# A hybrid decoder step: joining TensorE products that use part of the array, and another order for the first and the middle stretch

## The chip, the cores and the metric

One core of one Trainium2 chip. The time of a kernel is the device time of one execution in microseconds; the median of several runs is compared. All data is float32. "Full" products below use all 128 rows and 128 columns of TensorE's array.

## What is computed

A prompt of 512 rows and 8 sample rows (520 columns in the kernel's transposed layout, called T) go through two layers of width 1024. Cut to what matters here:

```python
def adaln(c, w, b):
    mod = (jax.nn.silu(c) @ w + b)[:, None, :]
    return jnp.split(mod, 3, axis=-1)          # shift, scale, gate

def even_layer(...):                            # layer 0
    h = rmsnorm(x, g) * (1 + scale) + shift
    z = h @ w_in                                # 8192 columns: conv parts, gates, q, k, v
    y_a = short_conv(...) * silu(ga)
    o = dilated_attn_prompt(q, k, v, slopes)    # or _decode, on 1024 cached keys and values
    out = concatenate([y_a, o * silu(gb)]) @ w_out
    return x + gate * out

def odd_layer(...):                             # layer 1
    h = rmsnorm(x, g) * (1 + scale) + shift
    z = h @ w_in                                # 6144 columns: u, gate, q, k, v, gate
    y_c = pool_mix(u, ...) * silu(gc)
    ret_new, o = retention_prompt(q, k, v)      # or retention_chunk on a state of 256 x 256 a head
    out = concatenate([y_c, norm(o) * silu(gd)]) @ w_out
    return x + gate * out
```

Both layers need adaLN's shift, scale and gate of 9 condition rows (8 samples, 1 prompt), and each is a product with a 1024 x 3072 matrix.

## The kernel before

**Tiles.** Activations are held transposed, 8 blocks of 128 features by 520 columns. A "tile" of work is one block of 128 output features: 8 blocks k, and in each three products (`mm3`, lines 295 to 302): high half of the weights by high and by low half of h, low half of the weights by high half of h, each over 256 and 264 columns, so 48 products. Halves come from a rounding on ScalarE (`whi`) and a subtraction on VectorE (`wlo`). Weights stream through four raw, three high and three low buffers (`w_raw`, `w_hi`, `w_lo`), asked for one tile ahead or more, all on SyncE's queue. There are 144 such tiles: 64 of layer 0's input projection, 16 of its output projection, 48 and 16 of layer 1.

**Order of the rest.** Everything else is hung between tiles by a clock written by hand: after each k of a tile `tick` (line 198) runs what is due, from four lists. `at` has fixed times; `put` is a heap of which one entry goes per tick; `put_fill` is a queue that is served when `put` has nothing due; `put2` goes every second tick. So one tick is 6 products of a tile, and the order on each engine is that of the calls. Engines run their own instructions strictly in order; a load on SyncE that waits for a buffer holds the loads behind it.

**What the change touches.**
- `H1A, H1B, DV, DK` (line 89): in ticks, when layer 1's blocks of h are scaled (H1A, and H1B between blocks) and how long the turning of v and k in the first retention head is put off (DV, DK), at the seam between the layers. There the first four tiles of layer 1 work on unscaled x (`z_first`), since the mean square is not known yet; `k_turn` (line 930, transposes on line 933) takes what ScalarE has made of such a tile.
- `ada_mm`, `ada_fin`, `ada` (lines 336 to 366): one adaLN block gives two column blocks. The condition is the stationary side, 32 columns of it, and the four column groups of the array (32 each) work on four k at once; the result is copied (`md`), turned and summed over the groups by a reduce, and its bias is added. Layer 0 has 8 blocks for shift and scale at the beginning and 4 for the gate during mixer A, layer 1 has 8 during the head pairs and 4 during layer 0's output projection. Each block is 1 MB in one of three `big` buffers.
- `score` (line 528) in `head_pair`: for a block of 128 queries and both heads e of a pair, three products each on 64 rows of the array; the two heads use the two halves of the rows. It is called four times a pair (8 pairs), for queries 0 to 3, and `soft` follows for each head.
- `window_weigh` (line 710): the sample rows' attention weights by cached values, on 32 columns of the array, four times.
- `state_read` (line 1054) in `ret_head`: q of the samples by the retention states, on 32 columns, twice a head, for samples 0 to 3 and 4 to 7.
- The beginning (lines 409 to 472): x is loaded, its mean square summed by products with a matrix of ones (`on_d`), the root's reciprocal taken on 520 columns, x multiplied by it on GpSimd, and then, in a loop over the blocks j, the adaLN block j is computed, h of block j - 1 is made, and the first two tiles take in block j - 2.
- `rms_sums`, `rms_roots`, `rms_rows` (lines 384 to 406): another way to the same root, with one-column products; before, only the seam uses it.

A float32 product runs as two passes on TensorE, so a profile counts two instructions for one; the products of tiles and scores are float32r and run as one.

Of the kernel before, what the change touches and what calls it, by code (L numbers as in the profile page):

```python
# [18 lines left out]
P = 128  # L19
D = 1024  # L20
KT = D // P
S = 512
# [64 lines left out]
def hybrid_kernel(ctx: ExitStack, tc: tile.TileContext, a, o):  # L87
    nc = tc.nc
    H1A, H1B, DV, DK = 11, 2, 6, 6
# [270 lines left out]
    def ada(layer, kind, j, raw=None):  # L360
        raw = raw or ada_load(layer, kind, j)

        def first():
            put_fill(ada_fin, layer, kind, j, ada_mm(raw), after=2)

        put_fill(first)
# [59 lines left out]
    sqa = tt()  # L426
# [6 lines left out]
    for x, first in ((sqa, True), (sq, False)):  # L433
        mm(ssq[0][:, 0:H0], on_d, x[:, 0:H0], first, not first)
        mm(ssq[1][:, 0:T - H0], on_d, x[:, H0:T], first, not first)
    act(r0[:, 0:H0], ssq[0][:, 0:H0], ACTF.Sqrt, bias=eps[:, 0:1])
    act(r0[:, H0:T], ssq[1][:, 0:T - H0], ACTF.Sqrt, bias=eps[:, 0:1])
    nc.vector.reciprocal(r0[:, 0:H0], r0[:, 0:H0])
    nc.vector.reciprocal(r0[:, H0:T], r0[:, H0:T])
    for x in xT:  # L440
        nc.gpsimd.tensor_tensor(out=x, in0=x, in1=r0, op=ALU.mult)
    for layer in range(2):
        o0 = PV[f"ada{layer}"] + 8
        vts(bsc[layer], pv[:, o0:o0 + 8], 1.0, None, ALU.add)
    h0, w01, ps01, hx = [], [], [mm2(), mm2()], {}

    for j in range(KT + 2):
        if j < KT:
            md = ada_mm(raw0[j])
        if 0 < j <= KT:  # L450
            hx[j - 1] = h_hi(0, j - 1, xT[j - 1][:, 0:S], xT[j - 1][:, S:T])
        if j < 2:
            w_hi()
        if j > 1:
            if not w01:
                w01 = [take_w(seq[0]), take_w(seq[1])]
            for w, ps in zip(w01, ps01):
                mm3(ps, w, j - 2, h0[j - 2][0], h0[j - 2][1], j == 2, j == KT + 1)
        if j < KT:
            ada_fin(0, "ss", j, md)  # L460
        if 0 < j <= KT:
            h0.append(h_lo(*hx.pop(j - 1)))
        if j < 2:
            w_lo()
        if j + 3 < KT:
            raw0.append(ada_load(0, "ss", j + 3))
        if j in (3, 5, 6):
            w_raw()
        if j == 6:
            w_hi()  # L470
            w_lo()
# [4 lines left out]
    QL = (0, 128, 256, 256)  # L476
    scores = tt(256).rearrange("p (t b h) -> p t b h", t=2, b=NB)
# [4 lines left out]
    def head_pair(p):  # L482
# [29 lines left out]
        def window_load():  # L512
# [6 lines left out]
            raw = ada_load(1, "ss", p)  # L519
            at(20, ada, 1, "ss", p, raw)  # L520
# [7 lines left out]
        def score(qb):  # L528

            N = max(H0, (qb + 1) * P)  # L530
            ss_ = [aux([P, S]) for _ in range(2)]
            for c, (x, y) in enumerate(((0, 0), (0, 1), (1, 0))):
                for e in range(2):
                    r = slice(64 * e, 64 * e + 64)
                    mm(ss_[e][:, 0:N], st["q"][x][r, qb * P:(qb + 1) * P], st["k"][y][r, 0:N], c == 0, c == 2)
            for e in range(2):
                soft(e, qb, ss_[e])
# [96 lines left out]
        for qb, n in enumerate((0, 2, 3, 5)):  # L634
            put(score, qb, after=Q0 + n)
# [74 lines left out]
    def window_weigh(b0):  # L710

        pd = aux([P, 512])
        for t in range(2):
            for u in range(2):
                for half in range(2):
# [4 lines left out]
                    )  # L720
        om = tt(512).rearrange("p (h d) -> p h d", d=64)
# [662 lines left out]
```

## Time and profile before

| | us |
|---|---|
| median of 3 runs | 1077.88 (1077.43 to 1079.83) |
| the profiled execution | 1079.61 |
| its span, first to last instruction | 1077.8 |
| third tile starts on TensorE | 52.47 |
| TensorE busy | 1044.0 |
| VectorE, ScalarE, GpSimd busy | 634.7, 492.4, 15.3 |

In the rows below, a timeline row is: start, duration, engine, line, operation, out<-in, shapes (active rows*columns of the array in front), count, and in brackets the idle time before it and what ended it. PE is TensorE, DVE VectorE, ACT ScalarE, POOL GpSimd, SPq SyncE's queue. `mm` is a tile's accumulator in PSUM, `aux` any other, `t` a buffer of 530 columns, `big` one of 2048. Line 160 is the helper of all products, 140 that of ScalarE, 146 that of VectorE with two tensors. A row of waits is: who waited for whom, total, times, longest.

### The profile page before, as it was taken

How to read it: one execution, taken by the hardware profiler on the slowest of the kernel's cores; microseconds unless marked ns; L12 is line 12 of the kernel's file. 1: busy time of each engine (PE TensorE's matmuls, PEld its weight loads, DVE VectorE, ACT ScalarE, POOL GpSimd, SP SyncE). 2: the span in 40 equal slices, each digit the busy share in tenths (PEclk: the TensorE clock that was granted, in tenths of full speed). 3: DMA queues.
4: the chain of work that ended last, by engine and by line, in shares of the span. 5: the costliest groups of instructions: out<-in, count | busy, mean ns of one | idle time of the engine just before them, and what ended most of it. 6: DMA issues, size and time to landing. Idle time of an engine off the chain costs nothing.

```text
span 1077.8 us, 21067 instructions
## 1 busy us (share of the span) xinstructions
PE 1044.0 (97%) x8668; PEld 991.3 (92%) x8668; DVE 634.7 (59%) x1477; ACT 492.4 (46%) x890; POOL 15.3 (1%) x37
## 2 busy tenths in 40 slices
PE   3999999999999999999999999999999999999996
PEld 1699999999989999999999999999999999999996
DVE  6556777667776445446344486565646667664443
ACT  5565676656663222224333465435454444333333
POOL 3000000000000000000000000000000000000000
PEclk8899999999999999999999999999999999999998
DMA  9386545665445365352744245272735533225222
GB/s 357 149 267 201 150 153 170 205 189 166 150 137 191 123 198 157 117 160 88 253 171 138 99 148 186 97 247 99 233 124 172 171 101 108 79 82 186 99 70 80
DMA packets 82176, 168.96 MB, mean 157 GB/s; under 512 B 7208, under 2 KB 47240, under 8 KB 79000
## 3 DMA queue, kind: packets, MB, share of 16 engines
q1 hardware_dynamic: 81792, 167.09, 47.7%
q8 instruction: 68, 1.11, 0.4%
q10 hardware_dynamic: 288, 0.52, 0.1%
q14 instruction: 28, 0.23, 0.1%
HBM read 149.40 MB, written 18.65 MB: 156 GB/s over the span
## 4 chain that ended last, share of the span: by engine, by line
PE 93%; DVE 4%; ACT 1%; issue 1%; DMA 0%; SPq 0%; DVEq 0%; ACTq 0%
PE mm L160 75%; PE aux L160 14%; PE aux L568 2%; DVE t L146 1%; ACT t L140 1%; DVE t L149 0%; PE aux L348 0%; DVE wlo L146 0%; PE aux L1254 0%; DMA t<-in_x_t 0%; PE aux L488 0%; PE aux L933 0%; DVE mA L154 0%; PE aux L926 0%; ACT whi L140 0%
## 5 line engine op out<-in xcount | busy, mean ns | idle before, releaser
L160 PE MATMUL mm<-t,whi 128*128 128x256 f32 (+1 forms) x4608 | 765.8, 288 | 6.8 <-ACT t L140 4.7
L160 PEld LDWEIGHTS mm<-t,whi 128*128 128x128 f32 x4608 | 638.4, 189 | 36.3 <-issue 22.1
L160 PE MATMUL mm<-t,wlo 128*128 128x256 f32 (+2 forms) x2304 | 466.3, 283 | 0.0
L160 PEld LDWEIGHTS mm<-t,wlo 128*128 128x128 f32 x2304 | 359.0, 189 | 0.0
L146 DVE TENSOR_TENSOR wlo<-wraw,whi 128x512 fp32r<-128x512 f32 x288 | 190.5, 691 | 51.8 <-ACT whi L140 51.2
L140 ACT ACTIVATE whi<-wraw 128x1024 fp32r<-128x1024 f32 x144 | 151.6, 1053 | 98.2 <-PE mm L160 62.9
L146 DVE TENSOR_TENSOR t<-t,t 128x520 fp32r<-128x520 f32 (+6 forms) x173 | 112.8, 655 | 95.1 <-ACT t L140 93.4
L140 ACT ACTIVATE t<-t 128x520 fp32r<-128x520 f32 (+3 forms) x116 | 71.0, 616 | 162.0 <-DVE t L149 97.3
L140 ACT ACTIVATE t<-aux 128x128 f32<-128x128 f32 (+7 forms) x149 | 68.4, 469 | 118.9 <-PE aux L160 67.9
L140 ACT ACTIVATE t<-mm 128x512 f32<-128x512 f32 (+2 forms) x116 | 56.3, 507 | 114.1 <-PE mm L160 112.6
L146 DVE TENSOR_TENSOR t<-aux,t 128x512 fp32r<-128x512 f32 (+6 forms) x120 | 60.8, 513 | 37.5 <-ACT t L140 32.2
L160 PE MATMUL aux<-t,t 64*128 64x256 f32 (+6 forms) x384 | 56.2, 329 | 0.0
L160 PE MATMUL aux<-t,v 128*128 128x512 f32 (+2 forms) x224 | 49.1, 324 | 0.7 <-DVE t L146 0.7
L546 DVE CUSTOM_DVE_ANT_0 t<-aux,t 128x128 f32<-128x128 f32 (+3 forms) x64 | 28.9, 489 | 31.9 <-PE aux L160 31.4
L160 PEld LDWEIGHTS aux<-t,t 64*128 64x128 f32 (+1 forms) x384 | 41.6, 187 | 5.4
L140 ACT ACT_TABLE_LOAD x32 | 41.1, 1283 | 1.3 <-PEq L1369 0.7
L140 ACT ACTIVATE t<-t,mn 128x128 f32<-128x128 f32 (+3 forms) x64 | 35.4, 554 | 13.3 <-DVE mn L546 13.1
L160 PEld LDWEIGHTS aux<-t,v 128*128 128x128 f32 x224 | 34.4, 188 | 1.9 <-DVE t L146 0.9
L149 DVE SCALAR_TENSOR_TENSOR big<-v,ksc,big 128x256 f32<-128x256 f32 x64 | 27.7, 481 | 10.1 <-ACT big L140 9.2
L350 DVE TENSOR_REDUCE m<-aux 128x18 f32<-128x72 f32 x24 | 5.6, 232 | 46.6 <-PE aux L348 46.6
L143 DVE COPY zs<-mm 128x8 f32<-128x8 f32 x76 | 12.1, 159 | 34.7 <-ACT t L140 29.1
L146 DVE TENSOR_TENSOR t<-mm,t 128x512 f32<-128x512 f32 (+1 forms) x24 | 16.5, 689 | 26.6 <-PE mm L160 17.4
(148 smaller groups left out, 585.6 us busy)
## 6 DMA issues: line engine op xcount, KB each, us to landing
wraw<-in_w_in_e SPq DMA_DIRECT2D x64, 512.0 KB, 7.1
wraw<-in_w_in_o SPq DMA_DIRECT2D x48, 512.0 KB, 3.3
big<-in_ada_e SPq DMA_DIRECT2D x12, 1024.0 KB, 8.3
big<-in_ada_o SPq DMA_DIRECT2D x12, 1024.0 KB, 10.0
wraw<-in_w_out_e SPq DMA_DIRECT2D x16, 512.0 KB, 3.8
big<-in_state_ret SPq DMA_DIRECT2D x16, 512.0 KB, 7.7
out_new_ret_sample<-big SPq DMA_DIRECT2D x16, 512.0 KB, 4.2
wraw<-in_w_out_o SPq DMA_DIRECT2D x16, 512.0 KB, 3.3
```

The source lines that it names most:

```text
L140: return nc.scalar.activation(out=out, in_=in_, func=func, scale=scale, **kw)
L143: return nc.vector.tensor_copy(out, in_)
L146: return nc.vector.tensor_tensor(out=out, in0=in0, in1=in1, op=op)
L149: return nc.vector.scalar_tensor_tensor(out=out, in0=in0, scalar=scalar, in1=in1, op0=op0, op1=op1)
L160: nc.tensor.matmul(out, lhsT=lhsT, rhs=rhs, start=start, stop=stop)
L350: nc.vector.tensor_reduce(out=m, in_=pt.rearrange("p s (g r) -> p s r g", g=4)[:, :, 0:9, :], op=ALU.add, axis=AX.X)
L546: nc.vector.tensor_tensor_reduce(out=sb, in0=s[:, 0:n], in1=bt[e][:, S - n:S], scale=1.0, scalar=3e38, op0=ALU.add, op1=ALU.min, accum_out=mn,
L568: nc.tensor.transpose(ep[:, c * P:(c + 1) * P], src, ident)
```

## The change

1. Joined products. `score` takes a list of query blocks; blocks 0 and 1 go into the two halves of one accumulator per head, one after the other, then come their `soft`. For layer 1, `ada_two` computes two adaLN blocks after each other into one accumulator and `ada_two_fin` finishes both. In layer 0 the gate's block j is computed inside `window_weigh`, right behind its products. `state_read` does all eight samples in one call.
2. The beginning. The mean square goes the way of the seam: one sum of squares on VectorE, one-column products, a root and reciprocal of five columns, and rows made by products. x is multiplied on VectorE, block by block inside the loop, GpSimd has nothing of it. `keep_warm` products, whose results nobody reads, stand after the squares of blocks 3 to 7 and in steps 1 and 2. Step j now does adaLN block j, the first two tiles' block j - 3, and h of block j. Two small loads come earlier, three weight loads one or two steps earlier.
3. The seam. H1A goes from 11 to 10, DV and DK from 6 to 8.

Cut to its core:

```diff
-    H1A, H1B, DV, DK = 11, 2, 6, 6
+    H1A, H1B, DV, DK = 10, 2, 8, 8
...
-    def ada(layer, kind, j, raw=None):
...
+    def ada_two(layer, kind, j, raws):
+        ps = aux([P, 4, P])
+        for c, raw in enumerate(raws):
+            for k in range(KT):
+                g = 32 * (k % 4)
+                mm(ps[g:g + 32, 2 * c:2 * c + 2], scT[:, k, :], raw[:, k], k < 4, k >= 4)
+        md = tt(4 * P).rearrange("p (s c) -> p s c", s=4)
+        act(md, ps)
+        put_fill(ada_two_fin, layer, kind, j, md, after=2)
...
     load(ct, a["c_t"])
+    load(csm[:, 0:P], a["c_small"][:, 0:P])
     xT = [tt() for _ in range(KT)]
     for j in range(KT):
         load(xT[j], a["x_t"][:, j, :])
-    load(csm[:, 0:P], a["c_small"][:, 0:P])
-    load(pv, a["small_t"])
+        if j == 1:
+            load(pv, a["small_t"])
...
+    def keep_warm(x, n):
+        ps = aux([P, H0])
+        for _ in range(n):
+            mm(ps, ident, x[:, 0:H0], True, True)
+
+    sqa, r0 = tt(), tt()
     for j in range(KT):
         sq = sqa if j == 0 else tt()
         act(sq, xT[j], ACTF.Square)
-        if 0 < j < KT - 1:
+        if j > 0:
             vtt(sqa, sqa, sq, ALU.add)
-    ssq, r0 = [aux([P, 512]) for _ in range(2)], tt()
...
-    nc.vector.reciprocal(r0[:, 0:H0], r0[:, 0:H0])
-    nc.vector.reciprocal(r0[:, H0:T], r0[:, H0:T])
-    for x in xT:
-        nc.gpsimd.tensor_tensor(out=x, in0=x, in1=r0, op=ALU.mult)
...
+        if j > 2:
+            keep_warm(xT[j], 2)
+    pc = rms_sums([sqa])
+    md = [ada_mm(raw0[0])]
+    rc = rms_roots(pc)
+    w_hi()
+    w_lo()
+    rms_rows(rc, r0)
+    vtt(xT[0], xT[0], r0, ALU.mult)
+    w_hi()
...
+    for j in range(KT):
+        if j > 0:
+            md.append(ada_mm(raw0[j]))
+        if j > 2:
+            first_two(j - 3)
+        elif j > 0:
+            keep_warm(xT[7], 2)
+        ada_fin(0, "ss", j, md[j])
         if j + 3 < KT:
             raw0.append(ada_load(0, "ss", j + 3))
+        hx = h_hi(0, j, xT[j][:, 0:S], xT[j][:, S:T])
+        if j + 1 < KT:
+            vtt(xT[j + 1], xT[j + 1], r0, ALU.mult)
+        h0.append(h_lo(*hx))
+        if j == 0:
+            w_lo()
...
-            raw = ada_load(1, "ss", p)
-            at(20, ada, 1, "ss", p, raw)
+            ada_w[p] = ada_load(1, "ss", p)
+            if p % 2:
+                at(20, put_fill, ada_two, 1, "ss", p - 1, (ada_w[p - 1], ada_w[p]))
...
-        for qb, n in enumerate((0, 2, 3, 5)):
-            put(score, qb, after=Q0 + n)
+        for blocks, n in (((0, 1), 0), ((2,), 3), ((3,), 5)):
+            put(score, blocks, after=Q0 + n)
...
+        mdg = ada_mm(ada_g.pop(b0 // 2))
+        put_fill(ada_fin, 0, "g", b0 // 2, mdg, after=2)
...
-        hook(4 + 5 * j, lambda j=j: ada_g.__setitem__(j, ada_load(0, "g", j)))
-        hook(6 + 5 * j, lambda j=j: ada(0, "g", j, ada_g.pop(j)))
+        hook(5 + 6 * j, lambda j=j: ada_g.__setitem__(j, ada_load(0, "g", j)))
...
-        if m < 4:
-            at(14, ada, 1, "g", m, ada_load(1, "g", m))
+        if m in (0, 2):
+            at(14, put_fill, ada_two, 1, "g", m, [ada_load(1, "g", m + i) for i in range(2)])
...
-        put(state_read, 0, after=6)
...
-                put(state_read, 4)
+                put(state_read)
```

How the order of the built program moves, at three places. TensorE in the first head pair before, at the score of query block 0 (`aux` the accumulators of the two heads, the two `t` on the right the halves of k), and where a tile goes on:

```order
L160 MATMUL aux_723<-t_558,t_677 128x256
L160 MATMUL aux_724<-t_558,t_677 128x256
L160 MATMUL aux_723<-t_559,t_677 128x256
L160 MATMUL aux_724<-t_559,t_677 128x256
L160 MATMUL aux_723<-t_558,t_678 128x256
L160 MATMUL aux_724<-t_558,t_678 128x256
L160 MATMUL mm_680<-t_417,whi_585 128x256
L160 MATMUL mm_680<-t_417,whi_585 128x264
```

And the same place in the changed kernel:

```order
L160 MATMUL aux_753<-t_588,t_707 128x256
L160 MATMUL aux_754<-t_588,t_707 128x256
L160 MATMUL aux_753<-t_589,t_707 128x256
L160 MATMUL aux_754<-t_589,t_707 128x256
L160 MATMUL aux_753<-t_588,t_708 128x256
L160 MATMUL aux_754<-t_588,t_708 128x256
L160 MATMUL aux_753<-t_588,t_707 128x256
L160 MATMUL aux_754<-t_588,t_707 128x256
L160 MATMUL aux_753<-t_589,t_707 128x256
L160 MATMUL aux_754<-t_589,t_707 128x256
L160 MATMUL aux_753<-t_588,t_708 128x256
L160 MATMUL aux_754<-t_588,t_708 128x256
```

Block 1's six products, which stood two ticks further on between products of a tile, follow block 0's without a full product between them.

TensorE in mixer A before, at the first weighing of cached values (`pT` the weights, `big` the values) between two k of a tile:

```order
L160 MATMUL mm_4486<-t_222,wlo_4359 128x264
L160 MATMUL aux_4493<-big_4308,pT 32x512 x2
L160 MATMUL aux_4493<-big_4312,pT 32x512 x2
L160 MATMUL aux_4493<-big_4308,pT 32x512 x2
L160 MATMUL aux_4493<-big_4312,pT 32x512 x2
L160 MATMUL mm_4486<-t_255,whi_4345 128x256
```

And in the changed kernel:

```order
L160 MATMUL mm_4454<-t_230,wlo_4345 128x264
L160 MATMUL aux_4461<-big_4292,pT 32x512 x2
L160 MATMUL aux_4461<-big_4296,pT 32x512 x2
L160 MATMUL aux_4461<-big_4292,pT 32x512 x2
L160 MATMUL aux_4461<-big_4296,pT 32x512 x2
L160 MATMUL aux_4470<-big_4300,scT 32x256 x8
L160 MATMUL mm_4454<-t_265,whi_4331 128x256
```

The gate's adaLN block (`scT` the condition), which stood alone in a tile of its own before, follows the weighing.

TensorE at the very beginning before (`on_d` the ones, `scT` an adaLN block, `md` its turning, then the first tile):

```order
L160 MATMUL aux_159<-t_137,on_d 128x256
L160 MATMUL aux_160<-t_137,on_d 128x264
L160 MATMUL aux_159<-t_157,on_d 128x256
L160 MATMUL aux_160<-t_157,on_d 128x264
L160 MATMUL aux_182<-big_125,scT 32x256 x8
L348 MATMUL aux_195<-csm,md_191 128x128 x2
L160 MATMUL aux_207<-big_129,scT 32x256 x8
L348 MATMUL aux_226<-csm,md_216 128x128 x2
L160 MATMUL aux_240<-big_133,scT 32x256 x8
L160 MATMUL mm_180<-t_222,whi_193 128x256
```

And in the changed kernel (the products of `t` with `csm` are `keep_warm`, those of `rc` make the rows):

```order
L160 MATMUL aux_175<-t_115,csm 128x256 x2
L160 MATMUL aux_178<-on_d,t_139 128x1 x5
L160 MATMUL aux_184<-big_125,scT 32x256 x8
L160 MATMUL aux_203<-csm,rc_195 128x128 x4
L160 MATMUL aux_209<-csm,rc_195 128x8
L348 MATMUL aux_217<-csm,md_193 128x128 x2
L160 MATMUL aux_238<-big_129,scT 32x256 x8
L160 MATMUL aux_249<-t_115,csm 128x256 x2
L348 MATMUL aux_252<-csm,md_247 128x128 x2
L160 MATMUL aux_270<-big_133,scT 32x256 x8
L160 MATMUL aux_281<-t_115,csm 128x256 x2
```

The sum over 520 columns has become one-column products behind five pairs of warming products, the rows are made between the first adaLN block and its turning, and the first tile's products come one step later in the loop.

More of the change, by code (lines that the diff above doesn't have):

```diff
@@ L358, in ada_fin, with ada_two_fin, cols @@
                 vts(mG[layer][:, 2 * j + s, :], m[:, s, :], pvc(f"ada{layer}", 16 + 2 * j + s), None, ALU.add)
-    def ada(layer, kind, j, raw=None):
[L361 to L366, printed above, removed]
+    def ada_two(layer, kind, j, raws):
[7 more added lines that the diff above has]
+        put_fill(ada_two_fin, layer, kind, j, md, after=2)
+    def ada_two_fin(layer, kind, j, md):
+        pt = aux([P, 4, P])
+        for s in range(4):
+            nc.tensor.transpose(pt[:, s, :], md[:, s, :], ident)
+        m = mk(cp, [P, 4, 9], F32, "m9x", 1)
+        nc.vector.tensor_reduce(
+            out=m, in_=pt.rearrange("p s (g r) -> p s r g", g=4)[:, :, 0:9, :], op=ALU.add, axis=AX.X
+        )
+        def cols(t, c, n):
+            return t[:, c:c + n].unsqueeze(2).to_broadcast([P, n, 9])
+        o = PV[f"ada{layer}"]
+        if kind == "ss":
+            s_ = slice(j, j + 2)
+            vtt(mS[layer][:, s_, 0:9], m[:, 0::2], cols(pv, o + j, 2), ALU.add)
+            vtt(m[:, 1::2], m[:, 1::2], cols(bsc[layer], j, 2), ALU.add)
+            vtt(mA[layer][:, s_, :], m[:, 1::2], cols(pv, PV[f"norm{layer}"] + j, 2), ALU.mult)
+        else:
+            vtt(mG[layer][:, 2 * j:2 * j + 4, :], m, cols(pv, o + 16 + 2 * j, 4), ALU.add)
     def h_hi(layer, j, xp, xs):
@@ L425, in hybrid_kernel @@
     act(warm, eps, ACTF.Sqrt)
-    sqa = tt()
+    for layer in range(2):
+        o0 = PV[f"ada{layer}"] + 8
+        vts(bsc[layer], pv[:, o0:o0 + 8], 1.0, None, ALU.add)
+    def keep_warm(x, n):
[3 more added lines that the diff above has]
+    sqa, r0 = tt(), tt()
     for j in range(KT):
@@ L438, in hybrid_kernel @@
-    nc.vector.reciprocal(r0[:, 0:H0], r0[:, 0:H0])
-    nc.vector.reciprocal(r0[:, H0:T], r0[:, H0:T])
-    for x in xT:
[L441 to L464, printed above, removed]
+        if j > 2:
+            keep_warm(xT[j], 2)
@@ L526, in q_load, with score @@
                 at(7 + 3 * t, put2, window_scores, t, st["kw"])
-        def score(qb):
-            N = max(H0, (qb + 1) * P)
+        def score(blocks):
             ss_ = [aux([P, S]) for _ in range(2)]
-            for c, (x, y) in enumerate(((0, 0), (0, 1), (1, 0))):
+            for qb in blocks:
+                N = max(H0, (qb + 1) * P)
+                c0 = H0 if qb == 1 else 0
+                for c, (x, y) in enumerate(((0, 0), (0, 1), (1, 0))):
+                    for e in range(2):
+                        r = slice(64 * e, 64 * e + 64)
+                        mm(
+                            ss_[e][:, c0:c0 + N], st["q"][x][r, qb * P:(qb + 1) * P], st["k"][y][r, 0:N],
+                            c == 0, c == 2,
+                        )
+            for i, qb in enumerate(blocks):
                 for e in range(2):
[L534 to L537, printed above, removed]
+                    soft(e, qb, ss_[e][:, i * H0:])
         def soft(e, qb, s):
@@ L1052, in state_store, with state_read @@
                 load(dst[:, :, k, :], st["sb", b0][:, :, k, :])
-        def state_read(b0):
-            if b0 == 0:
-                st["po"] = aux([P, 256])
-            for k in range(2):
-                for i in range(4):
-                    mm(
-                        st["po"][32 * i:32 * i + 32, :], qd[:, k, b0 + i, :], st["sb", b0][:, i, k, :],
-                        b0 == 0 and k == 0, b0 > 0 and k == 1,
-                    )
-            if b0 > 0:
-                st["pos"] = tt(256)
-                act(st["pos"], st["po"])
-                put(sample_out, after=4)
+        def state_read():
+            po = aux([P, 256])
+            for b0 in (0, 4):
+                for k in range(2):
+                    for i in range(4):
+                        mm(
+                            po[32 * i:32 * i + 32, :], qd[:, k, b0 + i, :], st["sb", b0][:, i, k, :],
+                            b0 == 0 and k == 0, b0 > 0 and k == 1,
+                        )
+            st["pos"] = tt(256)
+            act(st["pos"], po)
+            put(sample_out, after=4)
         def sample_out():
```

22 lines of the change are left out of this document (13 added, 9 removed).

## The prediction

> **What bounds the kernel now.** I read the page's busy times and its chain first, then the waits of TensorE, then its timeline at the places that the change edits, and last the first 55 us, engine by engine. From the page:
>
> ```profile
> PE 1044.0 (97%) x8668; PEld 991.3 (92%) x8668; DVE 634.7 (59%) x1477; ACT 492.4 (46%) x890; POOL 15.3 (1%) x37
> PE 93%; DVE 4%; ACT 1%; issue 1%; DMA 0%; SPq 0%; DVEq 0%; ACTq 0%
> ```
>
> TensorE is busy 97% of the span and carries 93% of the chain that ends last; VectorE stands at 59%. The waits of TensorE after the first 53 us:
>
> ```profile
> PE aux L160 <- DVE t L146: 3.1, 4, 1.0
> PE aux L933 <- ACT t L140: 2.0, 2, 1.0
> ```
>
> Three lines in all, and these two hold 5.1 us of it. So from 53 us on the kernel ends when TensorE has worked off its list, and a nanosecond taken from that list is a nanosecond of the time. Two things can be taken: time that TensorE loses inside the list without waiting for anybody, and the first 53 us, where it does wait.
>
> **Products on parts of the array.** The timeline of TensorE around one score of two heads (rows of 64 partitions), between full 128-row products:
>
> ```profile
> 201.67 0.28 PE L160 MATMUL mm<-t,wlo 128*128 128x264 f32 x1
> 201.88 0.62 PE L160 MATMUL aux<-t,t 64*128 64x256 f32 x6
> 202.43 0.75 PE L160 MATMUL mm<-t,whi 128*128 128x256 f32 x4
> 203.01 0.40 PE L160 MATMUL mm<-t,wlo 128*128 128x256 f32 x2
> 203.25 0.64 PE L160 MATMUL mm<-t,whi 128*128 128x256 f32 x4
> 203.73 0.28 PE L160 MATMUL mm<-t,wlo 128*128 128x256 f32 x1
> ```
>
> Starts are to be compared, since ends are modelled. Undisturbed, four products take 0.48 (203.25 to 203.73), 0.12 each. The last full product before the score holds TensorE 0.21 (201.67 to 201.88), 0.09 too long. The six score products run two at a time on the two halves of the array: three pairs at 0.12 would be 0.36; they take 0.55, 0.19 too long. The four full products after it take 0.58 (202.43 to 203.01), 0.10 too long. One stay on half the array so costs 0.38 beside its work. The same for one adaLN block (32 columns of the array, four products at a time), and for the weighing of cached values, whose products have the same count and twice the columns:
>
> ```profile
> 219.09 0.28 PE L160 MATMUL mm<-t,wlo 128*128 128x264 f32 x1
> 219.29 1.07 PE L160 MATMUL aux<-big,scT 128*32 128x256 f32 x16
> 220.29 0.75 PE L160 MATMUL mm<-t,whi 128*128 128x256 f32 x4
> 220.88 0.28 PE L160 MATMUL mm<-t,wlo 128*128 128x256 f32 x1
> ...
> 354.32 1.92 PE L160 MATMUL aux<-big,pT 128*32 128x512 f32 x16
> 356.17 0.62 PE L160 MATMUL mm<-t,whi 128*128 128x256 f32 x3
> ```
>
> 256 columns more cost 1.85 - 1.00 = 0.85, so the adaLN block's own work is 0.85 of its 1.00. The stay costs 0.08 ahead (0.20 against 0.12), 0.15 within and 0.11 behind (0.59 against 0.48): 0.34. What the change joins: scores of blocks 0 and 1, one stay fewer for each of 8 head pairs, 8 x 0.38 = 3.0. Layer 1's adaLN blocks two by two, 8 + 4 become 4 + 2, 6 x 0.34 = 2.0. Layer 0's four gate blocks go right behind the weighing of cached values, the same 32-column form, 4 x 0.34 = 1.4. The two state reads of each of four heads become one, of the same form, 4 x 0.34 = 1.4. Together 7.8. The work itself stays: as many products, transposes and columns. VectorE's combining of two adaLN blocks is one reduce of 36 columns and three small operations instead of two sets, hidden beside the 5.8 us of a tile (48 products at 0.12); uncovered it would be below 1 us each. Inside a stay pairs follow each other without a new cost as far as the rows show for one block; should the second block pay the 0.10 to 0.15 of a first group again, 22 x 0.10 to 0.15 = 2 to 3 come back. I take 7.8, with 5 to 8.5 as bounds.
>
> The Trainium skill ("TensorE: Matmul & The Clock Gate", section "Step-by-step: what each phase is for") gives the drain of the array as about 128 cycles; by an estimate of mine from that figure, at 2.4 GHz, a stay would cost two drains, 0.11 us, and the 22 stays 2.4, so that the whole sum would be 9.9. The rows above disagree with it by a factor of three, and the measurement decides.
>
> **The seam.** The second row of the waits is k's turning in the first retention head: twice 1.0 us in which TensorE waits for ScalarE's k. The change lets these turns come two ticks later, a tick being an eighth of a tile, 6 products or 0.72 us. 1.44 is more than 1.0, so both waits go: 2.0. The side list pops one step per tick and stays in order; nobody was late for v's turns, and v's way through DRAM ends 1.5 later, ahead of work that is due some 10 us on. The scaling of h1 one tick earlier frees nothing that TensorE waited for: 0. What is not settled by the edit is the clock there:
>
> ```profile
> 613.27 1.28 PE L160 MATMUL aux<-on_d,t 128*128 128x1 f32 x10 [1.04 <-DVE t L146]
> 614.41 1.19 PE L160 MATMUL mm<-t,whi 128*128 128x256 f32 x4
> 615.39 0.65 PE L160 MATMUL mm<-t,wlo 128*128 128x256 f32 x2
> ```
>
> ```profile
> 613.30:617.60 4.30, 4.30 (x25) 4.30 (x26) 1.54 (x4) 1.84 (x4) 0.00 (x0) 0.64 0.02 5
> ```
>
> After the wait for the sum of squares four products take 0.98, twice the 0.48, and the clock granted over these 4.30 us (the third number from the end, behind the busy times of PE, PEld, DVE, ACT and POOL) is 0.64: 3.1 us at half rate, 1.5 lost. Such a fall needs the gap to lie badly, and every edit before it shifts the gap: a gain of 0 to 1.5 for the range, 0 in the sum.
>
> **The beginning.** Rows of the timeline by engine, of the first 53 us:
>
> ```profile
> 6.11 4.01 ACT L140 ACTIVATE t<-t 128x520 f32<-128x520 f32 x6 [0.58 <-DMA t<-in_x_t]
> 6.78 3.92 DVE L146 TENSOR_TENSOR t<-t,t 128x520 f32<-128x520 f32 x5 [0.52 <-ACT t L140]
> 10.84 3.41 PE L160 MATMUL aux<-t,on_d 128*128 128x256 f32 x8 [10.84 <-DVE t L146]
> 15.98 1.75 DVE L439 RECIPROCAL t<-t 128x264 f32<-128x264 f32 x1
> 17.80 11.47 POOL L441 TENSOR_TENSOR t<-t,t 128x520 f32<-128x520 f32 x8 [16.34 <-DVE t L439]
> 20.12 1.56 PE L160 MATMUL aux<-big,scT 128*32 128x256 f32 x16 [1.83 <-DMA big<-in_ada_e]
> 25.82 0.80 PE L160 MATMUL mm<-t,whi 128*128 128x256 f32 x2 [4.13 <-ACT t L140]
> 27.44 0.69 DVE L146 TENSOR_TENSOR t<-t,t 128x520 fp32r<-128x520 f32 x1
> 38.43 1.07 PE L160 MATMUL aux<-big,scT 128*32 128x256 f32 x16
> 38.54 0.23 DVE L350 TENSOR_REDUCE m<-aux 128x18 f32<-128x72 f32 x1 [1.50 <-PE aux L348]
> 38.81 0.23 DVE L153 TENSOR_SCALAR mS<-m,pv 128x9 f32<-128x9 f32 x1
> 38.95 0.29 DVE L154 TENSOR_SCALAR mA<-m,bsc,pv 128x9 f32<-128x9 f32 x1
> 39.57 0.38 ACT L140 ACTIVATE md<-aux 128x256 f32<-128x256 f32 x1 [1.32 <-PE aux L160]
> 39.85 0.81 ACT L140 ACTIVATE t<-t,mS,mA 128x512 f32<-128x512 f32 x1
> 40.69 0.64 ACT L140 ACTIVATE t<-t 128x520 fp32r<-128x520 f32 x1
> 41.49 1.07 PE L160 MATMUL aux<-big,scT 128*32 128x256 f32 x16
> 52.47 0.74 PE L160 MATMUL mm<-t,whi 128*128 128x256 f32 x4 [0.17 <-DVE zs L143]
> ```
>
> Before: the root of x's mean square ends at 17.7, the first split block of h at 28.13 (27.44 + 0.69), eight blocks follow at 3.06 a step (38.43 to 41.49), and the third tile starts at 52.47. After, step by step. x waits for two small loads more (117 KB, 0.3 at the 420 GB/s of the row below), and VectorE adds one square more at 0.78: the sum of squares ends at 10.7 + 0.8 + 0.3 = 11.8. TensorE meanwhile runs the new warming products, 5 x 4 passes of the kind that takes 0.43 at half clock (8 in 3.41); from the arrival of x's fourth block (6.11 + 0.67 for one square + 0.3, so 7.1) they end at 15.5 if all are slow and at 13.0 if the clock rises after eight. I take 13.5. Then ten one-column passes (1.3, the row at the seam) to 14.8, the first adaLN block (1.07) and its copy (0.38) with hand-overs to 16.4; root and reciprocal of five columns, each like the 0.23 reduce, to 16.9; ten row products as at the seam to 18.2; their copy, at most 0.81, to 19.0; x times r, now on VectorE, 0.69, to 19.7; reduce, shift and scale 0.75 to 20.5; the three passes over h, 0.81 + 0.64 + 0.69, to 22.8. The first weight tile's split lies beside this. So the first block of h comes 5.3 sooner. Then step 1 takes about 4.0, since VectorE has the second weight tile's low half in its way; the other six go at the larger of TensorE's 3.06 and the ring that the new order closes (copy of the block 0.38, behind ScalarE's last pass; turning 0.3, combining 0.75, 0.81, 0.64, and five hand-overs): about 3.1. 22.8 + 4.0 + 6 x 3.1 = 45.4, the last 12 products 1.4, evacuation 0.2: third tile at 47.0 against 52.47. Gain 5.5. The multiplications leave GpSimd (11.47 for eight) for VectorE (8 x 0.69) at 2.5 of work per step, under the 3.1. Bounds: 2.5 with steps of 3.5, 8 with the warming products done at 13.0 and none of some 2 us of hand-overs in my chain. The loads do not bind: the fourth block's MB is asked for as soon as the first is used. The clock does something here:
>
> ```profile
> 18.00:22.00 4.00, 1.85 (x18) 0.64 (x17) 4.00 (x4) 0.81 (x1) 4.00 (x3) 0.82 1.02 420
> 22.00:26.00 4.00, 0.18 (x1) 0.19 (x2) 3.93 (x5) 0.87 (x2) 4.00 (x4) 0.50 1.01 414
> 34.00:38.00 4.00, 4.00 (x39) 3.09 (x38) 1.50 (x6) 2.26 (x5) 0.00 (x0) 0.97 0.94 348
> ```
>
> The columns are as at the seam. The clock fell inside the stretch in which TensorE was busy 1.85 of 4.00. After the change it is busy about half of 18 to 26, so a fall is possible; it would cost 1.5 where dense work resumes, as at the seam, which the bounds hold. The Trainium skill ("TensorE: Matmul & The Clock Gate", section "What's actually happening") has the clock halve after an idle window of about 3.4 us; by that rule the warming products keep it full and the sum stands, by the row it may be 1.5 less. This trace shows a fall after a stretch that was far from idle, and it decides: both stay open.
>
> **Sum.** 7.8 + 2.0 + 5.5 = 15.3. The profiled execution took 1079.6, its span 1077.8 and 1.8 around it: 1064.3 by that. The median of the runs is 1077.9, 1.7 lower: 1062.6. A difference under 0.2%, 2.2 us, cannot be told from none here.
>
> **Rivals.**
> *The beginning pays nothing* (0.17): the copy of each adaLN block now stands behind the passes over h in ScalarE's queue, so a step is a ring through three engines; 0.8 more on seven steps, 3.9, eats the 5.5. For it: step lengths of 4 in the first blocks of before. Against: those fell while GpSimd ran beside VectorE, and later steps had slack. 1077.9 - 9.8 = 1068.1.
> *Only the borders count* (0.07): the late first group after a border (0.10 on return, as much within) is weights that arrive late and would be late anyway; then a stay saves 0.18, 22 of them 4.0, and the time is 1077.9 - 11.5 = 1066.4. Against: undisturbed rows show no such lateness. The Trainium skill's figure of the drain, cited above, would put this rival at 1068.0.
> *The load queue blocks* (0.04, slower): the odd head's adaLN pair keeps an even head's 1 MB block for a whole head more. Three buffers rotate, so the cached keys of head p + 2 wait for that pair, and all weight loads behind them on SyncE. By the ticks the buffer is free 12 ticks, 8.7 us, before it is asked for, and two tiles of weights (11.6) lie ready. It decides only if the pair runs over 20 us late; then 6 a time at three heads, with 15.3 to eat: 1062.6 + 18 = 1080.6.
> *It does nothing measurable* (0.02): VectorE becomes the bound at the heads. At 59% it is not.
>
> **How the numbers follow.** The forecast has 0.70. The range: 8.5 + 2.0 + 1.5 + 8 = 20 at the good end, 1058; at the other end the beginning without gain, 1068.1, and 1 for joined stays that give a little less: 1058 to 1069. This holds the first three cases but their tails. Faster 0.94, same 0.02, slower 0.04.
>
> **What would show it.** Right: in a head's timeline twelve score products in one row with 0.9 to 1.0 from its start to the next full product; adaLN of layer 1 in rows of 32 passes, six in all; state reads in rows of 32, one a head; no wait of TensorE for k's turning in head 0; the third tile before 48. Wrong: a second 0.55 inside a joined row, steps over 3.5 at the beginning, new waits of TensorE on loads between 60 and 320 us.

## The result, and the profile after

The changed kernel takes 1068.97 us (median of 6 runs, 1066.22 to 1069.99), the kernel before 1077.66 on the same chip: ratio 0.9913, 95% interval 0.9897 to 0.9928. By the ratio it is faster by 9.4 (7.8 to 11.1), by the medians by 8.7, where 15.3 was forecast; the median lies 0.03 below the upper end of the range. The profiled execution took 1069.99, span 1068.1, so 9.6 less than that of before.

The engines' busy times, on the page of the kernel after:

```profile
PE 1044.3 (98%) x8708; PEld 997.9 (93%) x8708; DVE 626.8 (59%) x1470; ACT 491.3 (46%) x884; POOL 3.8 (0%) x29
```

TensorE is as busy as before (1044.0) although 22 stays are gone: 28 passes of warming products, counted as busy, came in, and something else that the experiments found. What TensorE waits for after 53 us (who, for whom, total, times, longest):

```profile
PE aux L160 <- DVE t L146: 2.4, 3, 1.1
PE aux L979 <- ACT t L140: 1.2, 2, 0.7
PE aux L160 <- DMA big<-in_ada_e: 1.1, 1, 1.1
PE aux L1298 <- DVE t L149: 0.6, 1, 0.6
```

k's turning (line 979 now) still waits, 1.2 in place of 2.0, and a wait for a load of layer 0's gate is new. The first row had 3.1 in four waits before; the one that is gone stood in the last head pair (0.65 at 323.88). The joined stays, in TensorE's timeline of the first heads:

```profile
178.90 1.93 PE L160 MATMUL aux<-big,scT 128*32 128x256 f32 x32
180.76 0.74 PE L160 MATMUL mm<-t,whi 128*128 128x256 f32 x4
...
195.96 0.98 PE L160 MATMUL aux<-t,t 64*128 64x256 f32 x12
196.87 0.75 PE L160 MATMUL mm<-t,whi 128*128 128x256 f32 x4
```

Twelve score products hold TensorE 0.91 from their start to the next full product, where two stays of six took 0.55 each: 0.19 less, and the other 0.19 is the second border. Two adaLN blocks take 1.86 in place of 2 x 1.00. Nothing is paid twice inside a row. Then the beginning, TensorE's timeline after:

```profile
8.14 7.53 PE L160 MATMUL aux<-t,csm 128*128 128x256 f32 x20 [8.14 <-DMA t<-in_x_t]
15.50 1.17 PE L160 MATMUL aux<-on_d,t 128*128 128x1 f32 x10
16.60 1.07 PE L160 MATMUL aux<-big,scT 128*32 128x256 f32 x16
18.65 1.25 PE L160 MATMUL aux<-csm,rc 128*128 128x128 f32 x10 [0.98 <-DVE rc L419]
...
23.86 0.44 PE L348 MATMUL aux<-csm,md 128*128 128x128 f32 x2 [1.63 <-ACT md L140]
24.23 1.82 PE L160 MATMUL aux<-big,scT 128*32 128x256 f32 x16
25.98 2.02 PE L160 MATMUL aux<-t,csm 128*128 128x256 f32 x4
27.92 0.44 PE L348 MATMUL aux<-csm,md 128*128 128x128 f32 x2
28.29 1.07 PE L160 MATMUL aux<-big,scT 128*32 128x256 f32 x16
...
31.30 1.07 PE L160 MATMUL aux<-big,scT 128*32 128x256 f32 x16
...
48.11 0.74 PE L160 MATMUL mm<-t,whi 128*128 128x256 f32 x4 [0.18 <-DVE zs L143]
```

The twenty warming passes run from 8.14 to 15.5, where the forecast had 7.1 to 13.5. Steps are 3.01 long (28.29 to 31.30). The passes at 24.23 and 25.98 took 1.07 and 1.13 elsewhere, here 1.82 and 2.02: half clock. The third tile starts at 48.11, 4.4 sooner than before.

### The profile page after: what moved, and what is told of

The parts are those of the page before. It is cut to its first block, busy times and chain, and to the rows that moved or that the text cites. A ratio compares the mean times of both kernels' runs of the same rounds, so it can differ in the third digit from the quotient of the medians.

```text
span 1068.1 us, 21092 instructions
## 1 busy us (share of the span) xinstructions
PE 1044.3 (98%) x8708; PEld 997.9 (93%) x8708; DVE 626.8 (59%) x1470; ACT 491.3 (46%) x884; POOL 3.8 (0%) x29
## 4 chain that ended last, share of the span: by engine, by line
PE 91%; DVE 2%; ACT 2%; DMA 1%; issue 0%; SPq 0%; DVEq 0%; ACTq 0%
PE mm L160 74%; PE aux L160 14%; ACT t L140 2%; PE aux L613 2%; DMA big<-in_ada_e 1%; DVE t L146 1%; DVE t L149 0%; PE aux L1298 0%; PE aux L348 0%; PE aux L526 0%; PE aux L979 0%; DVE wlo L146 0%; ACT whi L140 0%; PE aux L972 0%; PE aux L374 0%
## 5 line engine op out<-in xcount | busy, mean ns | idle before, releaser
L146 DVE TENSOR_TENSOR t<-t,t 128x520 fp32r<-128x520 f32 (+6 forms) x182 | 118.9, 657 | 96.1 <-ACT t L140 94.3
L140 ACT ACTIVATE t<-aux 128x512 f32<-128x512 f32 (+7 forms) x156 | 72.6, 475 | 135.0 <-PE aux L160 83.6
L146 DVE TENSOR_TENSOR gtmp<-mm,mG 128x8 f32<-128x8 f32 x16 | 2.6, 165 | 44.3 <-PE mm L160 44.3
## 6 DMA issues: line engine op xcount, KB each, us to landing
big<-in_ada_e SPq DMA_DIRECT2D x12, 1024.0 KB, 12.1
```

The source lines that it names most:

```text
L140: return nc.scalar.activation(out=out, in_=in_, func=func, scale=scale, **kw)
L146: return nc.vector.tensor_tensor(out=out, in0=in0, in1=in1, op=op)
```

## The experiments

Each is compared with the kernel before on its own chip, of which the median is in the last column of its group's first row. "Tile" is the time from the start of the 48th tile to that of the 49th, 48 full products with nothing between.

| kernel | median | ratio to before (95%) | third tile | tile, ns | before |
|---|---|---|---|---|---|
| changed kernel | 1068.97 | 0.9913 (0.9897 to 0.9928) | 48.11 | 5773 | 1077.66 |
| joined stays alone | 1070.36 | 0.9923 (0.9908 to 0.9938) | 53.22 | 5733 | 1078.93 |
| beginning alone | 1074.42 | 0.9965 (0.9952 to 0.9977) | 46.62 | 5773 | |
| old seam | 1068.42 | 0.9905 (0.9888 to 0.9921) | 47.16 | 5774 | |
| gate loads earlier | 1066.38 | 0.9884 (0.9868 to 0.9900) | 47.70 | 5773 | |
| ... without warming at squares | 1068.64 | 0.9915 (0.9900 to 0.9930) | 48.28 | 5774 | 1077.65 |
| ... with half of it | 1066.47 | 0.9895 (0.9878 to 0.9911) | 45.32 | 5773 | |
| ... k's turning later | 1065.70 | 0.9890 (0.9874 to 0.9906) | 48.23 | 5773 | |
| ... block 7 elsewhere | 1065.74 | 0.9886 (0.9870 to 0.9902) | 46.63 | 5733 | |
| all four together | 1065.02 | 0.9878 (0.9862 to 0.9893) | 45.42 | 5734 | 1077.93 |
| scores alone | 1075.98 | 0.9978 (0.9968 to 0.9988) | 51.90 | 5734 | |

The last two measures come from one profiled execution each, and the third tile's start moves between executions. Six kernels have the whole new beginning with all its warming products (the changed kernel, beginning alone, old seam, gate loads earlier, k's turning later, and, but for one small operation, block 7 elsewhere); in them it lies between 46.62 and 48.23. Their first product starts at 7.71 to 8.49, and their warming passes go from 0.43 to 0.22 each between 3.4 and 6.1 after that.

### The parts alone

Joined stays alone: the changed kernel with the beginning and the seam of before.

```diff
-    H1A, H1B, DV, DK = 10, 2, 8, 8
+    H1A, H1B, DV, DK = 11, 2, 6, 6
...
-    sqa, r0 = tt(), tt()
+    sqa = tt()
...
+    for x in xT:
+        nc.gpsimd.tensor_tensor(out=x, in0=x, in1=r0, op=ALU.mult)
```

> The changed kernel with the beginning and the four numbers of the seam as before: the joined products alone. Theory A (a stay on part of the array costs 0.34 to 0.38 us, the joined rows of the changed kernel's trace show it saved, and it comes off the time): 22 stays, 7.8 us less than before, minus the 1.1 to 1.3 us by which the gate's block is waited for behind the cached values: 6.5 less, about 1071. Theory B (what the stays save is given back by the full products around them, whose mean start to start rose from 119.4 to 120.2 ns in mixer A): about 3 less, 1074.5, and the same rise shows in this trace. Theory C (the rise belongs to the execution, not to the change): the time as in A, the rise may show or not.

Measured 1070.36, 8.6 less than before (interval 6.7 to 9.9 by the ratio). Theory B is out: plain products of layer 0 keep 119.3 ns. It is more than A's 6.5, and the trace has reasons for that: the waits for the gate's block cost 0.8 and not 1.1 to 1.3, the 0.65 of waiting in the last head pair is gone, and the clock doesn't fall at the seam, where half rate cost the kernel before 1.5. Beginning alone is the kernel before with the whole new beginning:

```diff
-    for x in xT:
-        nc.gpsimd.tensor_tensor(out=x, in0=x, in1=r0, op=ALU.mult)
...
+    pc = rms_sums([sqa])
+    md = [ada_mm(raw0[0])]
+    rc = rms_roots(pc)
```

> The kernel before with the new beginning alone. Theory A: its third tile starts near 48.1 as in the changed kernel, 4.4 us sooner, and the time is 4 to 4.5 less than before, 1073.3, more by up to 1.6 where the clock doesn't fall. Rival (part of the gain is lost later, because the weights of the next tiles come later in turn): under 3 less, with waits of TensorE on weights between 48 and 80 us.

Measured 1074.42, 4.5 less (2.5 to 5.2 by the ratio), although its third tile comes 5.85 sooner. It has no new wait of TensorE, and its clock did not fall at the beginning; 1.6 of the 5.85 are gone by the 67th tile. Whatever takes them stands in layer 0 and belongs to the new beginning alone.

Scores alone is the kernel before, with blocks 0 and 1 joined:

```diff
-        for qb, n in enumerate((0, 2, 3, 5)):
-            put(score, qb, after=Q0 + n)
+        for blocks, n in (((0, 1), 0), ((2,), 3), ((3,), 5)):
+            put(score, blocks, after=Q0 + n)
```

> The kernel before with the joined scores of query blocks 0 and 1 alone. Theory A, the price of a stay on half the array (0.38) holds for each of the eight head pairs: 3.0 less between the third tile and the output projection, addresses and all waits as before: 1074.7. Theory B, joining moves the scores ahead of other work and part of it comes back as waits for the attention's other steps: 0 to 1.5 less, 1076.5.

The starts of the third tile and of the 35th, on TensorE's timeline of this kernel:

```profile
51.90 0.74 PE L160 MATMUL mm<-t,whi 128*128 128x256 f32 x4 [0.17 <-DVE zs L143]
...
310.15 0.72 PE L160 MATMUL mm<-t,whi 128*128 128x256 f32 x4
```

And of the 35th in the kernel before:

```profile
313.80 0.60 PE L160 MATMUL mm<-t,whi 128*128 128x256 f32 x3
```

From third to 35th tile all eight head pairs are done: 258.25 here, 261.33 before (313.80 - 52.47). That is 3.08 for eight stays, 0.385 each: theory A, as far as this stretch goes. From the third tile to the last product 2.31 of it are left (1014.18 against 1016.49); the rest comes back in small pieces behind the heads, not as waits, and why is open. The median has 1.95 (0.9988 to 0.9968: 1.3 to 3.4), and the 3.0 lies in that interval. The Trainium skill ("TensorE: Matmul & The Clock Gate", section "Step-by-step: what each phase is for") has the array drain in about 128 cycles; two drains a stay, the estimate made ahead of the result, would have given 0.9 here, and the trace disagrees.

### The gate's load

```diff
-        hook(5 + 6 * j, lambda j=j: ada_g.__setitem__(j, ada_load(0, "g", j)))
+        hook(max(4, 2 + 6 * j), lambda j=j: ada_g.__setitem__(j, ada_load(0, "g", j)))
```

> The changed kernel with the gate's adaLN loads of layer 0 asked for three tiles before the cached values instead of behind them. Theory A (the 1.1 us wait for the gate's block is 3 MB that arrive last first served): the wait goes, 1 us less than the changed kernel, about 1068. Rival (the cached values themselves are then late, since the bytes stay): the wait stands before the cached values' products and the time is the same.

The edit asks for a block three tiles earlier, for the first of the four one tile. SyncE's queue in the changed kernel, with the load for the second gate block, and TensorE where it is used:

```profile
370.80 2.85 SPq L157 DMA_DIRECT2D big<-in_cache_win_v  x6
373.75 0.39 SPq L157 DMA_DIRECT2D big<-in_ada_e  x1
```

```profile
383.24 2.22 PE L160 MATMUL aux<-big,pT 128*32 128x512 f32 x16
386.56 1.07 PE L160 MATMUL aux<-big,scT 128*32 128x256 f32 x16 [1.11 <-DMA big<-in_ada_e]
```

The block is asked for behind six loads of cached values, 12.8 ahead of its use; the page gives such a block 12.1 from issue to landing as the median. With earlier loads the same place reads:

```profile
382.80 1.92 PE L160 MATMUL aux<-big,pT 128*32 128x512 f32 x16
384.54 1.05 PE L160 MATMUL aux<-big,scT 128*32 128x256 f32 x16
```

From the weighing's start to the block's: 3.32 before the edit, 1.74 with it. The load cost 1.6 here, more than the 1.1 of its row; the weighing's own row is longer too (2.22 against 1.92). It isn't the same in every execution: joined stays alone and the old seam, with the same loads, lose 0.8 and 1.1, at the second and the fourth of the four places. Nor does the edit take all of it away. Its trace at the fourth place:

```profile
460.12 2.31 PE L160 MATMUL aux<-big,pT 128*32 128x512 f32 x14
...
463.65 0.74 PE L160 MATMUL mm<-t,whi 128*128 128x256 f32 x4
```

That is 3.53 to the next full product, where the other three places take 2.72. Half of the warming and the four together lose 0.7 and 0.5 there, the other three kernels with this edit nothing. No wait is listed, but some of the weighing's products start late while the DMA engines are busy (0.88 or more of their time from 460.0 to 461.8). That fits the rival, by which the cached values then come late; no run separates it. So of 1.6 this trace keeps 0.8. Its last product starts 2.8 sooner than the changed kernel's (1056.39 against 1059.23): 0.8 by this, 0.4 by the third tile and 1.6 by the clock, which fell at the seam in the changed kernel (608.08) and not here. The median, 1066.38, is 2.6 below the changed kernel's, but the one execution of that kernel with as high a mean clock (0.998) took 1066.22: what the load is worth the medians don't show. The following kernels, marked with dots in the table, have this edit too.

### The seam

```diff
-    H1A, H1B, DV, DK = 10, 2, 8, 8
+    H1A, H1B, DV, DK = 11, 2, 6, 6
```

> The changed kernel with the four numbers of the seam as before (11, 2, 6, 6). Theory A (the later turns save what their waits got shorter, 2.3 - 1.5 = 0.8 us): 0.8 slower than the changed kernel, about 1069.8. Rival (the numbers do nothing, the waits are ScalarE's backlog and move with the turns): no difference. The waits before the two turns of k: 1.1 each by A.

Measured 1068.42, not to be told from the changed kernel. Its wait for k:

```profile
PE aux L979 <- ACT t L140: 2.1, 2, 1.1
```

These are A's waits, 0.9 more than in the changed kernel, which the medians can't show. The other way, k's turning two ticks later than in the changed kernel:

```diff
-    H1A, H1B, DV, DK = 10, 2, 8, 8
+    H1A, H1B, DV, DK = 10, 2, 8, 10
```

> The kernel with the earlier gate loads, and DK 10 in place of 8: k's turning in the first retention head two ticks (1.4) later still. Theory A, the price of the wait is only too short a delay: the two waits of TensorE for k (0.5 and 0.7 left) go, 1065.2, nothing else waits. Theory B, the backlog of ScalarE and VectorE at the seam goes with it: a wait of the same length stands at k or at the next thing turned there, 1066.4.

TensorE's waits there after 53 us:

```profile
PE aux L160 <- DVE t L146: 2.6, 4, 1.1
...
PE aux L160 <- ACT t L140: 0.2, 1, 0.2
PE mm L160 <- DVE zs L143: 0.2, 1, 0.2
```

With 6, 8 and 10 ticks TensorE waits 2.1, 1.2 and 0 for k: two ticks are 1.44 us and take away about 1 from a sum of two waits. At 10 three waits of 0.2 are new beside it (one of them in the first row, which was 2.4, 3), so 0.6 of the 1.2 is left as a gain, too little for the median (1065.70 against 1066.38) to show. Between the theories: most of the wait goes, half of it comes back as smaller ones.

### The warming products

```diff
-        if j > 2:
-            keep_warm(xT[j], 2)
```

> The kernel with the earlier gate loads (1066.4, third tile at 47.70), without the ten warming products between the squares; the warming products in steps 1 and 2 stay. Theory A, they cost what they were put there to save: VectorE's sum of squares is done at 12.60, TensorE gets to it at 15.07, so the sums start 2.5 sooner, the steps stay a ring of three engines at about 3.0, and the third tile starts at 45.2 to 45.7; time 1064. Theory B, they earn their keep: without them the granted clock stays at half through the first dense steps, where a step holds 12 full products (2.9 at half rate) and an adaLN block (2.1), together more than the 3.0 of the ring; two or three steps of 5 give back 3 to 5, third tile at 47.7 or later; time 1066.4 to 1069.

TensorE's beginning without them:

```profile
13.13 2.26 PE L160 MATMUL aux<-on_d,t 128*128 128x1 f32 x10 [13.13 <-DVE t L146]
15.32 1.93 PE L160 MATMUL aux<-big,scT 128*32 128x256 f32 x16
18.14 2.30 PE L160 MATMUL aux<-csm,rc 128*128 128x128 f32 x10 [0.89 <-DVE rc L419]
...
48.28 0.76 PE L160 MATMUL mm<-t,whi 128*128 128x256 f32 x4 [0.17 <-DVE zs L143]
```

The sums start 1.9 sooner than with them (15.07), and every step of the chain to the first h then takes twice as long: 2.26, 1.93 and 2.30 where 1.17, 1.07 and 1.25 stood. The third tile comes at 48.28, 0.6 later than with the earlier gate loads. Theory A falls; B has the outcome but not the place: the dense steps run at full clock (3.0 each), and it is the serial chain ahead of them that pays. With the products it lies between 46.62 and 48.23, so they pay for themselves, and that they gain anything isn't shown. The median, 1068.64, is 2.3 above that with the earlier gate loads; in the traces 1.6 of such a difference is the clock, which falls at the seam here (605.57) and not there. Half as many:

```diff
-            keep_warm(xT[j], 2)
+            keep_warm(xT[j], 1)
```

> The same kernel, with one warming product behind each of the squares of blocks 3 to 7 instead of two. At half clock ten passes of 0.43 from 8.10 are done at 12.4, just ahead of the sum of squares (12.60). Theory A: sums at 12.6, the clock rises some 6 us after TensorE begins, as it did with twice as many, so before the dense steps; third tile at 45.2, time 1064. Theory B: fewer products put the rise off into the steps; third tile at 46.5 to 48, time 1065.5 to 1067.

```profile
8.01 4.07 PE L160 MATMUL aux<-t,csm 128*128 128x256 f32 x10 [8.01 <-DMA t<-in_x_t]
12.63 1.25 PE L160 MATMUL aux<-on_d,t 128*128 128x1 f32 x10 [0.56 <-DVE t L146]
...
45.32 0.75 PE L160 MATMUL mm<-t,whi 128*128 128x256 f32 x4 [0.18 <-DVE zs L143]
```

That beginning reads so; ten passes end before the sum of squares, the sums run at full clock at 12.63, and the third tile comes 2.4 sooner, as A has it (1.3 sooner than the earliest with twenty). The median (1066.47) doesn't show it. The profiled execution was this kernel's fastest of four (1064.59, the others 1066.24 to 1066.85), that of the earlier gate loads its slowest (1067.15 of 1064.99 to 1067.15). Whether the gain is there in most executions stays open.

### Where the halves of h lie

What slows layer 0 with the new beginning is no wait. The starts of the 48th and the 49th tile before:

```profile
406.72 0.63 PE L160 MATMUL mm<-t,whi 128*128 128x256 f32 x4
...
412.45 0.40 PE L160 MATMUL mm<-t,whi 128*128 128x256 f32 x2
```

And after:

```profile
399.61 0.65 PE L160 MATMUL mm<-t,whi 128*128 128x256 f32 x4
...
405.39 0.28 PE L160 MATMUL mm<-t,whi 128*128 128x256 f32 x1
```

The same 48 products, nothing between them, 5.73 before and 5.78 after; the records give 5733 and 5773 ns, and each single product repeats to about a nanosecond from tile to tile. The table shows that the slow tile goes with the beginning, not with the joined stays, and the built programs show one thing that goes with it too: buffers are handed out in the order of use, and the new beginning gave the halves of h other addresses. Counted in buffers of 530 columns from block 0's high half, block 7's halves lay in 29 (high) and 18 (low), and now in 18 and 19. The experiment moves these back (what else stood in 29 goes to 19), by giving the low half an earlier first use:

```diff
         vtt(x[:, S:T], xs, mA[layer][:, j, 0:NB], ALU.mult)
+        lo = tr() if (layer, j) == (0, 7) else None
+        if lo is not None:
+            vtt(lo[:, S:T], xs, mA[layer][:, j, 0:NB], ALU.mult)
```

> The kernel with the earlier gate loads, with one VectorE product of eight columns more in the beginning (overwritten later), by which the halves of h's block 7 lie at other addresses: high half in slot 29 of the 530-column buffers, low half in 18, as in the kernel before, in place of 18 and 19; every other address is as it was. Theory A, the plain products of layer 0 run slower in the changed kernel because of where the halves of h lie: the six products of block 0, which follow block 7's, go from 731 ns back to 701, a tile of 48 products from 5758 ns to about 5730, and 62 tiles save 1.6 to 1.9; mean from start to start 119.4 in place of 120.0, time 1064.7. Theory B, the pace goes with something else in the new beginning (when weights are loaded or split, traffic of the other engines): 731 ns and 120.0 stay, 1066.4.

```profile
395.92 0.64 PE L160 MATMUL mm<-t,whi 128*128 128x256 f32 x4
...
401.65 0.40 PE L160 MATMUL mm<-t,whi 128*128 128x256 f32 x2
```

5.73 again, with one small VectorE operation more and the operands of all other products where they were: theory A. Most of it lies in the six products of block 0, which follow block 7's (731 ns, 710 here, 701 before), and of block 1 (722, 708, 719). Over all tiles of layer 0 the mean from start to start goes from 120.0 to 119.6 ns, where before had 119.4: 0.4 x 48 x 62 = 1.2 us of the 0.6 x 48 x 62 = 1.8 that were lost. What in the addresses does it isn't settled, and the medians (1065.74 against 1066.38) cannot show 1.2.

### All four together

Gate loads, one warming product, block 7's place, DK 10: the edits above in one kernel.

> The changed kernel with four edits: gate loads three hooks earlier, one warming product per square, block 7's halves at the other addresses, DK 10. From the traces of each alone: the gate's wait 1.1, third tile 2.4 sooner, layer 0's plain products 1.2, k's waits 0.5, in all 5.2. Theory A, these are separate pieces of one list of TensorE and add up: 1066.4 (gate loads alone) - 4.1 = 1062.3. Theory B, what is won ahead is given back behind, by a window at half clock (1.6) or a new wait at the seam: 1064 to 1066.

Measured 1065.02, ratio 0.9878 (0.9862 to 0.9893): faster than the changed kernel (0.9897 to 0.9928), not to be told from the earlier gate loads alone, and nearer to theory B. In its trace each piece is there (third tile 45.42, tile 5734, no wait for k or for the gate), but the fourth weighing takes 0.5 too long, and a stretch at half clock stands at the seam:

```profile
601.90:605.30 3.40, 3.40 (x18) 3.40 (x18) 0.91 (x4) 0.54 (x2) 0.00 (x0) 0.52 0.00 0
```

3.4 us at half rate, some 1.5 lost. The kernel with k's turning later and the one with the earlier gate loads had no such stretch there; the changed kernel, the old seam, the one without warming at the squares and the one with block 7 elsewhere had one. So the fall isn't shown to come from putting the four together, and that the pieces add up but for it is not ruled out.

## Why the prediction was right or wrong

Forecast and measurement, in us of the profiled executions (the first row is a remainder, so the sum checks nothing; the scores alone do):

| step | forecast | measured | from |
|---|---|---|---|
| 22 stays fewer | 7.8 | 7.2 | what is left of 9.7 with the others taken off; scores alone 3.08 for 3.0 |
| a wait in the last head pair | 0 | 0.7 | first row of the waits, 3.1 and 2.4 |
| the gate's load | 0 | -1.6 | the two fences on it |
| the seam | 2.0 | 0.8 | waits 2.0 and 1.2 |
| the beginning | 5.5 | 4.4 | third tile 52.47 and 48.11 |
| plain products of layer 0 | 0 | -1.8 | 119.4 and 120.0 ns |
| sum | 15.3 | 9.7 | last product starts 9.7 sooner; 9.6 by the times |

**Joined stays: right**, mechanism and size. The price of 0.38, read from starts around one stay, held for all eight head pairs. For the 32-column stays the joined row (1.86 for 2.00) and the remainder fit 0.34; no run has them alone. The wait that went with them (it is gone in joined stays alone and stands in scores alone) had no term in the sum. The rival that only the borders count is out: the 0.19 inside a score stay is saved as well. That TensorE's busy time didn't fall is the warming products and the slower plain ones.

**The gate's four blocks: the step that failed.** "Layer 0's four gate blocks go right behind the weighing" was costed as a stay less, without asking when its load is issued. The text checked the buffers of layer 1's pairs and looked for load waits up to 320 us; the wait came at 385, one block of four, and took 1.6, more than the 1.4 that the four stays gave (0.8 and 1.1 in the two other traces with these loads).

**The seam: the step "1.44 is more than 1.0, so both waits go".** The delay was taken off each wait as if k's makers stayed where they were: two ticks took 0.9 off the 2.1. As I read the order on ScalarE and VectorE, v's turn, put off as well, comes between and pushes k's steps back; that is argued, and no run moved k's turning alone from 6 to 8.

**The beginning: mechanism right, one term mis-sized.** Steps of 3.1 were 3.01. The warming products, taken to run from 7.1 to 13.5, ran from 8.14 to 15.5: x came 1.0 later than reckoned, and fourteen of the twenty passes went at half rate, where eight would have ended at 13.0. From their end to the third tile it was 32.6 where 33.5 was forecast. Beginning alone, in which eight passes were slow, ended them at 13.99 and had its third tile at 46.62, 32.6 later too. Its rows:

```profile
13.99 1.17 PE L160 MATMUL aux<-on_d,t 128*128 128x1 f32 x10
...
22.36 0.44 PE L348 MATMUL aux<-csm,md 128*128 128x128 f32 x2 [1.63 <-ACT md L140]
...
26.42 0.44 PE L348 MATMUL aux<-csm,md 128*128 128x128 f32 x2 [1.56 <-ACT md L140]
```

The fall of the clock in steps 1 and 2, which the bounds had at 1.5, cost nothing. From one turning of a block to the next it is 4.06 here with the clock kept, and 4.06 in the changed kernel (23.86 to 27.92); the slow passes fill the 1.56 in which TensorE otherwise waits for ScalarE's copy. The windows of the fall:

```profile
20.00:24.40 4.40, 2.77 (x28) 1.45 (x30) 3.67 (x11) 3.08 (x5) 0.00 (x0) 1.00 0.97 346
...
20.99:24.40 3.41, 1.78 (x14) 1.04 (x14) 2.77 (x9) 2.09 (x4) 0.00 (x0) 1.00 0.96 327
24.40:27.80 3.40, 3.40 (x20) 1.61 (x12) 2.76 (x9) 1.66 (x3) 0.00 (x0) 0.50 0.48 157
```

These are of the kernel after, with columns as in the prediction. The clock falls right after 3.41 us in which TensorE was busy for 1.78, warming products included. The rule of the Trainium skill ("TensorE: Matmul & The Clock Gate", section "What's actually happening") that it takes an idle window of 3.4 us does not hold here; that its window is free-running, as the same section says, would fit the next observation. With the earlier gate loads the same stretch holds as much work (2.77 of 4.40, the first row above and below) and the clock stays:

```profile
20.00:24.40 4.40, 2.77 (x34) 1.47 (x30) 3.67 (x12) 2.64 (x4) 0.00 (x0) 1.00 0.96 372
24.40:27.80 3.40, 1.84 (x18) 0.88 (x6) 2.76 (x9) 1.72 (x3) 0.00 (x0) 1.00 0.68 248
```

That kernel's four executions all had a mean clock of 0.998, the changed kernel's six 0.994 to 0.998.

**Plain products: no step at all.** The prediction took 0.12 a product as given. The change left the products alone and moved their operands.

The rival that the beginning pays nothing gave 1068.1, next to the 1068.97 measured, and is wrong all the same: the beginning's ring did not slow (3.01), and alone it paid 3.8 to 4.5. The number came from two losses elsewhere. That the median fell inside the range by 0.03 is luck as well: its upper end allowed for a beginning without gain, and what brought the time there were the gate's load and the plain products, for which the sum had no term.

## What to carry to other kernels

When work is moved up to save a border, look up when its load is asked for and how long that load takes, beside the buffers. A wait on an engine with a backlog doesn't shrink by the whole delay that it is given. A gain of a few tenths of a per cent can be made or lost by addresses and by where the clock falls, so count undisturbed tiles in the trace before a mechanism is credited or blamed for it.

## What the runs showed of the hardware

- 48 plain products of 256 and 264 columns took 5773 ns, and 5733 with block 7's two operand buffers at other addresses.
- At the start passes take twice their time (0.43) while the granted-clock record says 1.00. Six kernels with the same beginning left that state 3.4 to 6.1 us after their first product.

```profile
8.10:14.10 6.00, 5.96 (x14) 4.83 (x15) 4.12 (x6) 3.11 (x5) 0.00 (x0) 1.00 1.03 411
```

- A fall of the clock lasted 3.4 us in the changed kernel and in the four together (13.65 at the beginning of the kernel before). It followed 3.41 us in which TensorE was busy for 1.78 (above) or, at the seam of the four together, 2.36. With the earlier gate loads TensorE was busy for 2.36 of 3.41 ahead of the same place as well, and the clock stayed full behind it. First the four together, then the earlier gate loads:

```profile
598.49:601.90 3.41, 2.36 (x20) 2.15 (x19) 1.94 (x5) 2.55 (x5) 0.00 (x0) 0.97 0.38 150
...
600.83:604.24 3.41, 2.36 (x20) 2.15 (x18) 1.75 (x5) 1.25 (x2) 0.00 (x0) 1.00 0.63 221
```
